# Output pieces split by adding transfers, and narrower first products, in a decoder layer on one core

## The chip, the core and the metric

The kernel runs on one core of one Trainium2 chip. The core has five engines that run side by side and wait for one another by semaphores: TensorE (PE, with its weight loads shown apart as PEld), VectorE (DVE), ScalarE (ACT), GpSimd (POOL) and SyncE (SP, which only issues transfers here). POOL can issue transfers too, among them such as add to what stands in on-chip memory. The metric is the time of one execution on the device in microseconds (us). Before the change the median of three runs is 2339.99 us (2338.28 to 2340.84).

## The reference

One decoder layer on 256 tokens of width 2048, all in float32. What matters here:

```
h = layer_norm(ALPHA * h + 0.5 * swiglu(h, ffn1_w_in, ffn1_w_out), ln1_g, ln1_b)
p = h @ w_in                      # q, k, v, indexer, recurrent branch, gates
merged = g_attn * (dsa_attention(...) @ w_attn_branch) + g_rnn * (rglru_branch(...) @ w_rnn_branch)
h = layer_norm(ALPHA * h + merged @ w_out, ln2_g, ln2_b)
h = layer_norm(ALPHA * h + 0.5 * swiglu(h, ffn2_w_in, ffn2_w_out), ln3_g, ln3_b)

def swiglu(h, w_in, w_out):
    a, b = split(h @ w_in, 2)     # inner width 5632
    return (silu(a) * b) @ w_out
```

Nearly all of the work is products of 256 tokens with weights that are read once. The two FFNs hold most of the weights.

## The kernel before

**Three products for one.** A float32 number is kept as two rounded halves, h (its rounding) and l (the rest). A product of tokens and weights is three products on PE: token h by weight h, token h by weight l, token l by weight h. That is `three` (lines 742 to 745); lines 743, 744 and 745 are therefore the commonest rows of the profile. The tokens are the stationary operand (128 by 128, loaded anew for every product), the weights stream by as 512 or 256 columns.

**Pieces.** All weights form one list of pieces in the order of their use, and `Weights` keeps three places in it: where PE is (`cur`), how far pieces are split into halves (`cur + AHEAD`, 4), and how far they are loaded (8). There are four kinds:

- a plain piece `c` of an FFN's input weights, 1024 columns: twelve products of 512 columns, streamed as two rows of 512;
- a form: a chunk of 2048 columns of the input weights is used in four forms (`p1q3`, `p2`, `q5p7`, `q4p6`), which are sums of its quarters (Strassen's scheme in Winograd's variant). They cost DVE additions (lines 230, 234, 237), and save products. A chunk's forms are 42 products of 256 columns, six (p2) or twelve (the others) a form;
- an output piece `o` of an FFN's output weights, 1024 columns, which fill in between (twelve products of 512 columns);
- pieces of the other stages, of the same shapes.

A piece is split by ACT, which writes h (line 275), and DVE, which subtracts it from the piece and writes l (line 276), into one of five buffers `hl`. A chunk of 2048 columns is loaded into one of three buffers `rf`, other pieces into one of four `raw`.

**Far pieces.** Some output pieces go another way, so that DVE does nothing for them: the far pieces (`far_to`, lines 167 to 187). Their loads are issued when the piece is `EARLY + LOADS` = 16 pieces ahead of PE, their split 12 ahead. ACT writes minus the rounded piece into two tiles `wd` (line 182), POOL issues for each a transfer that reads the piece from memory once more and adds it (line 183), which leaves l; ACT writes h into two further tiles (line 185). In each FFN the output weights are worked off in groups of 4 pieces (k = 0, 2, 4, 6: one segment of the inner width and one quarter of the outputs); far are those with k = 2 and 6 (in the first, shorter segment only k = 2, and for two quarters). That is 34 pieces in each FFN.

**Order.** The order on PE, SP and POOL is that of the program text. On ACT and DVE a scheduler sets it when the kernel is built. An FFN has 22 blocks of 256 inner columns; the last sixteen use four chunks each, with one group of output pieces: three pieces first, then eight forms, the fourth piece, and eight forms. The block's gate (lines 1132 to 1145) is worked off on ACT and DVE while the next block's output pieces run, and its result is turned on PE by four transpositions (line 1151). Other stages mix the same kinds of pieces, with fewer chunks in forms.

`run` (in `blockF`) issues the products of one half form: `three` twice, for two rows of 256 columns. `tokens` calls `three` for the 512-column pieces.

Of the kernel before, what the change touches and what calls it, by code (L numbers as in the profile page):

```python
# [16 lines left out]
S = 256  # L17
# [45 lines left out]
AHEAD = 4  # L63
EARLY = 12
LOADS = 4
FORMS = ("p1q3", "p2", "q5p7", "q4p6")
PIECE = 1024
FAST = (0, 1, 2, 3)
# [69 lines left out]
class Weights:  # L138
# [28 lines left out]
    def far_to(self, i):  # L167


        nc = self.nc  # L170
        while self.far_loaded < len(self.far) and self.far[self.far_loaded] <= i + LOADS:
            k = self.far[self.far_loaded]
            ap = self.pieces[k][0]
            t = self.far_raw[k] = self.pool.tile([P, PIECE], F32, name=f"raw{k}", tag="raw", bufs=RAW_BUFS)
            nc.sync.dma_start(t, ap)
            self.far_loaded += 1
        while self.far_split < len(self.far) and self.far[self.far_split] <= i:
            k = self.far[self.far_split]
            ap, t = self.pieces[k][0], self.far_raw.pop(k)
            h, l = ([self.wide() for _ in range(2)] for _ in range(2))  # L180
            for c in range(2):
                nc.scalar.activation(l[c], t[:, c * 512:(c + 1) * 512], AF.Copy, scale=-1.0)
                nc.gpsimd.dma_start(l[c], ap[:, c * 512:(c + 1) * 512], accum_op=OP.add)
            for c in range(2):
                nc.scalar.activation(h[c], t[:, c * 512:(c + 1) * 512], AF.Copy)
            self.hl[k] = (h, l)
            self.far_split += 1
# [180 lines left out]
def tile_layer(ctx, tc, x_fm, x_tm, pos, f1a, f1o, wA, wki, wB, wG, lru, wab, wrb, wo, f2a, f2o,  # L368
# [46 lines left out]
    def block_pieces(ap, plan, fills=None, fo=None):  # L415
        chunk = {}
        for f, k in plan:
            if f == "c":
                pieces.append((ap[:, k * 512:k * 512 + PIECE], None))
            elif f == "o" and not fo:  # L420
                plain([next(fills)])
            elif f == "o":
                g, nb, k = next(fills)
                if k in (2, 6) and (g or nb >= 2):
                    far.append(len(pieces))
                k += 2 * SEGS[g][0]
                pieces.append((fo[nb][:, k * 512:k * 512 + PIECE], None))
            else:
                if k not in chunk:
                    chunk[k] = ap[:, k * 2048:(k + 1) * 2048]  # L430
                pieces.append((chunk[k], f))
# [30 lines left out]
    for i in range(NR + LAG):  # L462
# [4 lines left out]
        if i >= LAG:  # L467
            g, c = divmod(i - LAG, TPG)
# [273 lines left out]
    def three(ps, xh, xl, w, start, stop):  # L742
        T.matmul(ps, xh, w[0], start=start, stop=False)  # L743
        T.matmul(ps, xh, w[1], start=False, stop=False)  # L744
        T.matmul(ps, xl, w[0], start=False, stop=stop)  # L745

    def tokens(ps, x, t, w, start, stop):
        three(ps, x[:, 0, t * P:(t + 1) * P], x[:, 1, t * P:(t + 1) * P], w, start, stop)

    def eager(hs, ps):  # L750
# [28 lines left out]
    def blockF(x, forms, plan, fill):  # L779
# [14 lines left out]
        for i, (form, k) in enumerate(plan):  # L794
            if i < skip:
                continue
            if form == "o":
                fill()
                continue
            if not c:  # L800
                c = [MM(), MM()]
            start, stop = ([f.get(b) == i for b in range(4)] for f in (first, last))
            if form == "c":
                for j in (k, k + 1):
                    w = W.unit(512)
                    for t in range(2):
                        tokens(c[t], x[j], t, w, start[t] and j == k, stop[t] and j > k)
                continue
            if not e:
                e = [BP(), BP()]  # L810
            c11, c12, c21 = c[0][:, :S], c[0][:, S:], c[1][:, :S]
            p1, p6, p7, q5 = e[0][:, :S], e[0][:, S:], e[1][:, :S], e[1][:, S:]
            fs = [forms[2 * k + r] for r in range(2)]

            def xop(i, t):
                return [tuple(x[4 * k + 2 * r + i][:, a, t * P:(t + 1) * P] for a in range(2)) for r in range(2)]

            def sop(i):
                return [tuple(v[:, i * P:(i + 1) * P] for v in fs[r]) for r in range(2)]

            def run(ps, ops, start, stop):
                for r in range(2):
                    three(ps, *ops[r], W.unit(S), start and r == 0, stop and r == 1)

            if form == "p1q3":
                run(p1, xop(0, 0), start[2], stop[2])
                run(c12, sop(3), start[0], stop[0])
            elif form == "p2":
                run(c11, xop(1, 0), start[0], stop[0])
            elif form == "q5p7":  # L830
                run(q5, sop(0), start[3], False)
                run(p7, sop(2), False, stop[3])
            else:
                run(c21, xop(1, 1), start[1], stop[1])
                run(p6, sop(1), start[2], stop[2])
# [288 lines left out]
    def ffn(x, forms, ln):  # L1124
        def gate(c, e, g, i, lag, plain):
# [20 lines left out]
            for _ in range(lag):  # L1146
                yield
            ps = BP()
            for k in range(2):
                for t in range(2):  # L1150
                    T.transpose(ps[:, k * S + t * P:k * S + (t + 1) * P], z[:, t * 512 + k * P:t * 512 + (k + 1) * P], ident)
# [544 lines left out]
```

## Time and profile before

| | |
|---|---|
| median of the runs | 2339.99 us |
| profiled execution | 2340.27 us, its span 2338.4 us |
| PE busy | 2312.5 us (99%), 15430 products and as many weight loads |
| DVE busy | 2201.5 us (94%) |
| ACT busy | 1560.0 us (67%) |
| POOL busy | 263.4 us (11%) |
| read from memory, written | 507.10 MB, 37.22 MB |
| granted clock of PE | 1.000 |

The first FFN runs to about 705 us, the input projections, attention and the recurrent branch follow, and the second FFN begins at about 1640 us. Rows of the profile name the line, the engine, the operation, what it writes and reads (`out<-in`, numbers of buffers left out) and the size. In rows of groups stand the count, the busy time with the mean of one in ns, and the engine's idle time before them with what ended it. In rows in order of time stand the start, the duration of the row (all of its instructions, where it ends in xN) and, in brackets, idle time before it. A product lasts longer than the step to the next one, since products are pipelined: what a product costs is the step from start to start. Rows of stretches give the busy time of the engines in each, the clock, the share of the DMA engines' time and the rate.

### The profile page before, as it was taken

The page shows a single profiled execution, that of the slowest core. Times are in us where ns is not written, and L with a number is a line of the kernel's source. Part 1 is how long each engine was busy: PE and PEld are TensorE (multiplying, and loading weights), DVE is VectorE, ACT ScalarE, POOL GpSimd, SP SyncE. Part 2 cuts the span into 40 slices and gives each one's busy share as a digit, 9 for nine tenths or more (in the row PEclk, how much of TensorE's full clock was granted, in tenths as well). Part 3 has the DMA queues.
Part 4 walks back from the last instruction along what each step waited for, and adds up shares of the span by engine and source line. Part 5 has one row for each costly group of instructions (what it writes and reads, how often), then busy time and mean ns, then how long its engine had stood idle before and what let it go on. Part 6 is the DMA issues. An engine that isn't in the chain of part 4 may idle for free.

```text
span 2338.4 us, 40427 instructions
## 1 busy us (share of the span) xinstructions
PE 2312.5 (99%) x15430; PEld 2109.4 (90%) x15430; DVE 2201.5 (94%) x3196; ACT 1560.0 (67%) x2273; POOL 263.4 (11%) x368
## 2 busy tenths in 40 slices
PE   9999999999999999999999999999999999999998
PEld 7899999999988999888899998888889999999997
DVE  7999999999999999979887888998999999999997
ACT  7667777777757656556557785555667777777763
POOL 1101111111110000000100001100111111111111
PEclk9999999999999999999999999999999999999999
DMA  9878988888876556554675658655788888888875
GB/s 336 251 238 240 261 250 251 250 256 250 230 244 209 192 187 216 185 189 154 244 239 193 200 182 326 239 198 195 242 275 232 253 255 252 243 252 267 244 221 215
DMA packets 142178, 546.97 MB, mean 234 GB/s; under 512 B 16640, under 2 KB 17280, under 8 KB 117536
## 3 DMA queue, kind: packets, MB, share of 16 engines
q1 hardware_dynamic: 100800, 455.00, 55.1%
q0 software_dynamic: 41040, 89.27, 18.4%
q8 instruction: 120, 1.97, 0.3%
q14 instruction: 74, 0.61, 0.1%
q10 hardware_dynamic: 144, 0.13, 0.0%
HBM read 507.10 MB, written 37.22 MB: 233 GB/s over the span
## 4 chain that ended last, share of the span: by engine, by line
PE 66%; DVE 23%; issue 5%; DMA 3%; ACT 2%; POOL 0%; SPq 0%; ACTq 0%; DVEq 0%; POOLq 0%
PE mm L743 13%; PE mm L745 13%; PE mm L744 13%; DVE hl L276 13%; PE bp L744 5%; PE bp L745 5%; PE bp L743 4%; PE mm L1390 3%; PE mm L1389 3%; PE mm L1391 3%; DVE ws L230 2%; DVE rf L237 2%; DVE rf L234 2%; ACT hl L275 2%; DMA raw<-f1o 1%
## 5 line engine op out<-in xcount | busy, mean ns | idle before, releaser
L275 ACT ACTIVATE hl<-rf 128x1024 fp32r<-128x1024 f32 x573 | 511.3, 912 | 232.9 <-DVE rf L237 119.7
L276 DVE TENSOR_TENSOR hl<-rf,hl 128x1024 fp32r<-128x1024 f32 x573 | 596.9, 1047 | 8.2 <-ACT hl L275 3.8
L276 DVE TENSOR_TENSOR hl<-raw,hl 128x1024 fp32r<-128x1024 f32 (+3 forms) x402 | 474.2, 1196 | 62.2 <-ACT hl L275 61.4
L275 ACT ACTIVATE hl<-raw 128x1024 fp32r<-128x1024 f32 (+3 forms) x402 | 408.4, 1035 | 179.4 <-PE mm L745 82.8
L744 PE MATMUL bp<-hl,sh 128*128 128x256 f32 x1146 | 323.6, 282 | 10.1 <-DVE hl L276 10.1
L743 PE MATMUL bp<-hl,sh 128*128 128x256 f32 x1146 | 320.9, 280 | 0.0
L745 PE MATMUL bp<-hl,sl 128*128 128x256 f32 x1146 | 320.2, 279 | 0.0
L743 PE MATMUL mm<-hl,hs 128*128 128x512 f32 (+1 forms) x800 | 274.5, 343 | 1.6 <-DVE z L1139 0.7
L275 ACT ACTIVATE hl<-ws 128x1024 fp32r<-128x1024 f32 x191 | 202.0, 1058 | 102.7 <-DVE ws L230 71.5
L744 PE MATMUL mm<-hl,hs 128*128 128x512 f32 (+1 forms) x800 | 268.3, 335 | 0.0
L745 PE MATMUL mm<-hl,hs 128*128 128x512 f32 (+1 forms) x800 | 267.9, 335 | 0.1
L230 DVE TENSOR_TENSOR ws<-rf 128x1024 f32<-128x1024 f32 x191 | 233.8, 1224 | 5.4 <-DMA rf<-wrb 1.3
L276 DVE TENSOR_TENSOR hl<-ws,hl 128x1024 fp32r<-128x1024 f32 x191 | 234.2, 1226 | 1.8 <-ACT hl L275 1.7
L744 PEld LDWEIGHTS bp<-hl,sh 128*128 128x128 f32 x1146 | 215.4, 188 | 17.5 <-DVE hl L276 16.3
L745 PEld LDWEIGHTS bp<-hl,sl 128*128 128x128 f32 x1146 | 217.7, 190 | 0.0
L743 PEld LDWEIGHTS bp<-hl,sh 128*128 128x128 f32 x1146 | 215.4, 188 | 1.3
L1389 PE MATMUL mm<-hs,hl 128*128 128x256 f32 x640 | 178.3, 279 | 0.0
L1391 PE MATMUL mm<-hs,hl 128*128 128x256 f32 x640 | 177.8, 278 | 0.0
L1390 PE MATMUL mm<-hs,hl 128*128 128x256 f32 x640 | 177.7, 278 | 0.0
L743 PEld LDWEIGHTS mm<-hl,hs 128*128 128x128 f32 x800 | 150.4, 188 | 19.1 <-issue 2.6
L745 PEld LDWEIGHTS mm<-hl,hs 128*128 128x128 f32 x800 | 151.0, 189 | 16.7 <-DVE hs L937 0.5
L744 PEld LDWEIGHTS mm<-hl,hs 128*128 128x128 f32 x800 | 150.5, 188 | 14.3 <-DVE hl L276 0.2
(360 smaller groups left out, 5897.6 us busy)
## 6 DMA issues: line engine op xcount, KB each, us to landing
rf<-f1a SPq DMA_DIRECT2D x75, 1024.0 KB, 7.7
rf<-f2a SPq DMA_DIRECT2D x75, 1024.0 KB, 7.5
raw<-f1o SPq DMA_DIRECT2D x88, 512.0 KB, 6.6
raw<-f2o SPq DMA_DIRECT2D x88, 512.0 KB, 6.6
raw<-wB SPq DMA_DIRECT2D x80, 512.0 KB, 4.8
raw<-wG SPq DMA_DIRECT2D x54, 512.0 KB, 4.2
ya<-yd POOLq DMA_DIRECT2D x80, 256.0 KB, 7.4
rf<-wA SPq DMA_DIRECT2D x20, 1024.0 KB, 5.5
```

Source lines behind the costliest of these rows:

```text
L230: v.tensor_tensor(t, b[:, 0:4:3], b[:, 1:2].to_broadcast([P, 2, 2, 256]), op=OP.add)
L234: v.tensor_tensor(b[:, 1], t[:, 1], b[:, 0], op=OP.add)
L237: v.tensor_tensor(b[:, 0], b[:, 1], b[:, 2], op=OP.add)
L275: nc.scalar.activation(hp, src, AF.Copy)
L276: self.last = nc.vector.tensor_tensor(lp, src, hp, op=OP.subtract)
L743: T.matmul(ps, xh, w[0], start=start, stop=False)
L744: T.matmul(ps, xh, w[1], start=False, stop=False)
L745: T.matmul(ps, xl, w[0], start=False, stop=stop)
L1389: T.matmul(ps[:, :S], w[0], x[:, 0], start=first, stop=False)
L1390: T.matmul(ps[:, :S], w[0], x[:, 1], start=False, stop=False)
L1391: T.matmul(ps[:, :S], w[1], x[:, 0], start=False, stop=last)
```

## The change

There are two edits. First, output pieces with k = 4 are far pieces too, so that three of four in every group of the longer segments are split by adding transfers, and far pieces are loaded eight pieces ahead of their split instead of four. Second, where a form's products follow products of 512 columns, the first of them is issued as two products of 128 columns, with the same stationary operand. A mark, `after_wide`, is set by `tokens` when it streams 512 columns, and cleared by a form's products and by the transpositions of a gate.

```diff
 LOADS = 4
+FAR_LOADS = 8
@@ far_to
-        while self.far_loaded < len(self.far) and self.far[self.far_loaded] <= i + LOADS:
+        while self.far_loaded < len(self.far) and self.far[self.far_loaded] <= i + FAR_LOADS:
@@ block_pieces
-                if k in (2, 6) and (g or nb >= 2):
+                if k in (2, 4, 6) and (g or nb >= 2):
                     far.append(len(pieces))
@@ beside three
+    after_wide = [False]
+
+    def entry(ps, xh, xl, w, start, stop):
+        n = w[0].shape[1] // 2
+        for c in range(2):
+            T.matmul(ps[:, c * n:(c + 1) * n], xh, w[0][:, c * n:(c + 1) * n], start=start and c == 0, stop=False)
+        T.matmul(ps, xh, w[1], start=False, stop=False)
+        T.matmul(ps, xl, w[0], start=False, stop=stop)
+
     def tokens(ps, x, t, w, start, stop):
+        after_wide[0] = w[0].shape[1] == 512
         three(ps, x[:, 0, t * P:(t + 1) * P], x[:, 1, t * P:(t + 1) * P], w, start, stop)
@@ run, in blockF
-                    three(ps, *ops[r], W.unit(S), start and r == 0, stop and r == 1)
+                    w = W.unit(S)
+                    (entry if after_wide[0] else three)(ps, *ops[r], w, start and r == 0, stop and r == 1)
+                    after_wide[0] = False
@@ gate, before its transpositions
+            after_wide[0] = False
```

The built programs show what this moves. Names below carry the number of the piece, so `hl301` is piece 301; rows of the change have its own line numbers, one to fifteen above the old ones. Piece 298 is the first of a group of output pieces (k = 0), 299 and 300 follow (k = 2 and 4), 301 is the next block's first form, 309 the group's fourth piece.

On PE, at the step from piece 300 to piece 301, before:

```order
L743 MATMUL mm376_5655<-hl300_5601,g303_4349 128x512
L744 MATMUL mm376_5655<-hl300_5601,g303_4349 128x512
L745 MATMUL mm376_5655<-hl300_5601,g303_4349 128x512
L743 MATMUL bp379_5705<-hl301_5628,xs10_132 128x256
L744 MATMUL bp379_5705<-hl301_5628,xs10_132 128x256
```

and now:

```order
L744 MATMUL mm424_5772<-wd413_5589,g335_4433 128x512
L745 MATMUL mm424_5772<-wd415_5591,g335_4433 128x512
L746 MATMUL mm424_5772<-wd413_5589,g335_4433 128x512
L753 MATMUL bp427_5826<-hl301_5745,xs10_132 128x128 x2
L754 MATMUL bp427_5826<-hl301_5745,xs10_132 128x256
```

Piece 300 is read from the tiles `wd` of a far piece, and the first product of piece 301 is two of 128 columns. There are 154 such pairs in the program.

On DVE, at the same place of the list, where a group's output pieces are split, before:

```order
L276 TENSOR_TENSOR hl297_5565<-rf294_5438,hl297_5565 128x1024
L276 TENSOR_TENSOR hl298_5580<-raw298_5514,hl298_5580 128x1024
L276 TENSOR_TENSOR hl300_5601<-raw300_5543,hl300_5601 128x1024
L230 TENSOR_TENSOR ws301_5629<-rf301_5563 128x1024
L1133 TENSOR_TENSOR z374_5645<-z374_5645,bp359_5351 128x256
L276 TENSOR_TENSOR hl301_5628<-rf301_5563,hl301_5628 128x1024
```

and now:

```order
L277 TENSOR_TENSOR hl297_5685<-rf294_5549,hl297_5685 128x1024
L277 TENSOR_TENSOR hl298_5700<-raw298_5637,hl298_5700 128x1024
L231 TENSOR_TENSOR ws301_5746<-rf301_5683 128x1024
L277 TENSOR_TENSOR hl301_5745<-rf301_5683,hl301_5745 128x1024
L235 TENSOR_TENSOR rf301_5683<-ws301_5746,rf301_5683 128x2x256
```

The subtraction for piece 300 is gone; the gate's first addition (z) now stands behind the sums of the form.

On ACT, in the middle of that block, where the far pieces of the next group are split (319, and now 320 as well), before:

```order
L182 ACTIVATE wd386_5807<-raw319_5736 128x512
L182 ACTIVATE wd387_5808<-raw319_5736 128x512
L185 ACTIVATE wd384_5805<-raw319_5736 128x512
L185 ACTIVATE wd385_5806<-raw319_5736 128x512
L275 ACTIVATE hl311_5815<-rf310_5724 128x512
L275 ACTIVATE hl312_5831<-ws310_5795 128x1024
```

and now:

```order
L276 ACTIVATE hl311_5935<-rf310_5846 128x512
L183 ACTIVATE wd434_5927<-raw319_5789 128x512
L183 ACTIVATE wd435_5928<-raw319_5789 128x512
L186 ACTIVATE wd432_5925<-raw319_5789 128x512
L186 ACTIVATE wd433_5926<-raw319_5789 128x512
L183 ACTIVATE wd438_5953<-raw320_5807 128x512
L183 ACTIVATE wd439_5954<-raw320_5807 128x512
L186 ACTIVATE wd436_5951<-raw320_5807 128x512
L186 ACTIVATE wd437_5952<-raw320_5807 128x512
L276 ACTIVATE hl312_5961<-ws310_5915 128x1024
L276 ACTIVATE hl313_5979<-rf310_5846 128x1024
```

Eight conversions of far pieces stand in a row there, ahead of `hl312`, where it had four, ahead of `hl311`. This is so in eight of the 32 blocks; in the others they stand in groups of three to five.

## The prediction

> **What bounds the kernel now.** I read the page first, then the busy time by stretch, the waits of TensorE (PE), and the order of time at a few places.
>
> ```profile
> span 2338.4 us, 40427 instructions
> PE 2312.5 (99%) x15430; PEld 2109.4 (90%) x15430; DVE 2201.5 (94%) x3196; ACT 1560.0 (67%) x2273; POOL 263.4 (11%) x368
> ...
> PE 66%; DVE 23%; issue 5%; DMA 3%; ACT 2%; POOL 0%; SPq 0%; ACTq 0%; DVEq 0%; POOLq 0%
> ```
>
> PE and VectorE (DVE) share the chain that ended last. Which of them binds depends on the stage, so the averages are split by stretch: thirteen equal blocks of the first FFN, fourteen of the second, and the recurrent branch for contrast.
>
> ```profile
> core 0: us, PE busy (x) PEld busy (x) DVE busy (x) ACT busy (x) POOL busy (x), PEclk, DMA share, GB/s
> 249.80:658.80 409.00, 404.57 (x2861) 377.27 (x2861) 407.14 (x494) 292.93 (x409) 69.72 (x82) 1.00 0.85 248
> 1840.90:2280.60 439.70, 435.33 (x3080) 405.88 (x3080) 438.18 (x533) 315.45 (x442) 73.83 (x86) 1.00 0.84 248
> 1100.00:1380.00 280.00, 280.00 (x2225) 267.93 (x2224) 232.58 (x353) 190.73 (x286) 13.94 (x26) 1.00 0.63 212
> ```
>
> In the FFN blocks DVE is busy 407.14 of 409.00 us, while PE is idle for 4.4: DVE sets their period, 409.00/13 = 31.46 us. From 1100 to 1380 PE never rests and DVE has 47 us to spare. So work taken from DVE can pay only in the FFN blocks, and work added to PE costs everywhere unless PE waits.
>
> How much PE waits for DVE stands in the waits, and at one place of each block in the order of time.
>
> ```profile
> PE bp L744 <- DVE hl L276: 10.1, 30, 0.6
> ```
> ```profile
> 375.04 0.28 PE L743 MATMUL bp<-hl,sh 128*128 128x256 f32 x1
> 375.71 0.38 PE L744 MATMUL bp<-hl,sh 128*128 128x256 f32 x1 [0.39 <-DVE hl L276]
> 375.93 0.28 PE L745 MATMUL bp<-hl,sl 128*128 128x256 f32 x1
> ...
> 376.40 0.28 PE L743 MATMUL bp<-hl,sh 128*128 128x256 f32 x1
> ...
> 378.32 0.28 PE L745 MATMUL bp<-hl,sl 128*128 128x256 f32 x1
> 378.44 0.39 PE L743 MATMUL mm<-hl,g 128*128 128x512 f32 x1
> ```
>
> There are thirty waits, one per block, at the last form ahead of the output pieces, 10.1 us of idle time. One costs more than its idle time: the two starts after 375.04 take 0.89 us where two products take 0.23, so 0.66 against 0.39 idle. Taken over the thirty places in the same way, 14.3 us. That is the most that relief of DVE can return here.
>
> **Two pitches of one product.** The seventeen starts from 376.40 to 378.32, behind that wait, are 0.113 us apart. Behind 512 columns the same product goes slower:
>
> ```profile
> 305.02 0.39 PE L745 MATMUL mm<-wd,g 128*128 128x512 f32 x1
> 305.25 0.28 PE L743 MATMUL bp<-hl,xs 128*128 128x256 f32 x1
> 305.36 0.28 PE L744 MATMUL bp<-hl,xs 128*128 128x256 f32 x1
> ...
> 308.66 0.28 PE L745 MATMUL bp<-hl,sl 128*128 128x256 f32 x1
> ```
>
> From 305.25 to 308.66 are 29 steps, 0.1177 us each. The state holds: of 143 stretches of eight and more that begin behind 512 columns, 141 keep the slow pitch to their end (a wait, transpositions, or 512 columns). It is 4.4 ns a product. Transpositions, 128 columns wide, usually end it:
>
> ```profile
> 91.30 0.60 PE L1151 MATMUL bp<-ident,z 128*128 128x128 f32 x4
> 91.65 0.37 PE L743 MATMUL mm<-hl,xs 128*128 128x256 f32 x1
> 91.85 0.28 PE L744 MATMUL mm<-hl,xs 128*128 128x256 f32 x1
> 91.97 0.28 PE L745 MATMUL mm<-hl,xs 128*128 128x256 f32 x1
> ...
> 92.43 0.28 PE L743 MATMUL bp<-hl,sh 128*128 128x256 f32 x1
> ```
>
> **The change, part by part.** *Entries.* 154 products of 256 columns become two of 128 (64 in the 32 four-chunk blocks, two each; 90 elsewhere), each with a weight load of its own, as every product here has (15430 of both on the page). No row shows a rounded product of 128 columns. The nearest are the transpositions above and the plain float32 products of attention:
>
> ```profile
> L1151 PE MATMUL bp<-ident,z 128*128 128x128 f32 x176 | 26.4, 272 | 0.0
> ```
> ```profile
> 1001.05 0.39 PE L1354 MATMUL bp<-hT,hT 128*128 128x128 f32 x2
> 1001.27 0.60 PE L1355 MATMUL bp<-hT,hT 128*128 128x256 f32 x2
> ```
>
> Four transpositions take 0.60 us and one lasts 0.27, so 0.11 a step; two plain products step on in 0.22, again 0.11 each. The upper bound is the slow pitch, 0.118, if each load waits as it does there. Two steps replace one of 0.118: plus 0.100 (from 0.109) to 0.118. I take 0.105, nearer to these rows because of the width: 154 x 0.105 = 16.2 us (15.4 to 18.2), all on PE. The Trainium skill ("TensorE: Matmul & The Clock Gate", section Back-to-back issue gap) gives about 81 ns for a 128-column product in a stream of weight loads and products; by that the pair would add 44 ns, 6.8 us in all, and the sum below would be 2318 us. The trace disagrees for this data: 0.11 us in both rows above.
>
> What the entry may return: from each of the 154 places to the next wait, transposition or 512 columns I count 4,563 products in the trace (the first place at 55.67 us, the last at 2273.04), which at 4.4 ns are 20.0 us. The lower bound is nothing. Behind the transpositions the pitch needs some five products to fall to 0.113 (0.12, 0.12, 0.11 from 91.85), about 2 us over all places: 18. Whether the new pair ends the slow state is the open question. Of 38 waits inside such a stream, a step of chance length, 27 come out at 0.113 (376.40 above) and 11 at 0.118, such as this one:
>
> ```profile
> 407.36 0.39 PE L744 MATMUL bp<-hl,sh 128*128 128x256 f32 x1 [0.52 <-DVE hl L276]
> ...
> 409.71 0.28 PE L745 MATMUL bp<-hl,sl 128*128 128x256 f32 x1
> ```
>
> Transpositions straight behind 512 columns end it in four of seven cases. So I give the pair about six in ten; timing behind 512 columns repeats, so it should be nearly all places or nearly none.
>
> *Three of four pieces.* 32 more pieces (sixteen an FFN, one a block) lose their split on DVE and get four conversions on ScalarE (ACT) and two adding transfers.
>
> ```profile
> L276 DVE TENSOR_TENSOR hl<-raw,hl 128x1024 fp32r<-128x1024 f32 x385 | 464.6, 1223 | 59.1 <-ACT hl L275 58.4
> ...
> 345.46 2.35 DVE L276 TENSOR_TENSOR hl<-raw,hl 128x1024 fp32r<-128x1024 f32 x2
> ...
> 344.19 1.99 ACT L275 ACTIVATE hl<-raw 128x1024 fp32r<-128x1024 f32 x2
> 346.09 1.56 ACT L275 ACTIVATE hl<-rf 128x1024 fp32r<-128x1024 f32 x2
> ...
> 363.30 1.14 ACT L182 ACTIVATE wd<-raw 128x512 fp32r<-128x512 f32 x2
> 364.34 1.14 ACT L185 ACTIVATE wd<-raw 128x512 fp32r<-128x512 f32 x2
> ```
>
> DVE: two subtractions step on in 2.35 - 1.22 = 1.13 us, so a block needs 31.32 - 1.13 = 30.19 us of DVE (407.14/13 = 31.32). PE without its wait needs 31.46 - 0.48 = 30.98, and with two entries 31.19, or 30.9 with the pitch returned. DVE then has 0.7 to 1.0 us to spare in a block, and PE becomes the bound. The wait of 14.3 us goes; I count 80%, 11.4 us, since the relief is small and DVE's gate chain still comes in one burst. ACT: four conversions at 0.52 (364.34 - 363.30 over two) for one of 0.95: plus 1.13 us on 22.5 of 31.46, hidden as a sum. But the order puts eight of them in a row in eight blocks, 4.2 us, ahead of two conversions of a form; elsewhere up to five, 2.6 us.
>
> ```profile
> L182 ACT ACTIVATE wd<-raw 128x512 fp32r<-128x512 f32 x136 | 78.2, 620 | 2.7 <-DMA raw<-f2o 2.1 <-DMA raw<-f1o 0.5
> ...
> L183 POOL DMA_DIRECT2D wd<-f1o x68 | 71.7, 1380 | 335.4 <-ACT wd L182 248.3 <-PE bp L745 65.4 <-DVE g L879 21.7
> ```
> ```profile
> wd<-f1o POOLq DMA_DIRECT2D x68, 256.0 KB, 9.5
> ...
> rf<-f1a SPq DMA_DIRECT2D x75, 1024.0 KB, 7.7
> ```
>
> ACT did wait for these loads, 2.7 us in all; issuing them four pieces earlier (some 5 us) removes that and puts them ahead of chunk loads in SP's queue, whose buffers turn over with DVE and which land in 7.7 us. POOL issues two more transfers a block, 2 x 1.38 us beside 5.3 busy of 31.46: hidden. They land in 9.5 us and are used more than a dozen pieces after their load. The transfers add 0.52 MB to 248 GB/s x 31.46 us = 7.8 MB a block, so the DMA share goes from 0.85 to about 0.91.
>
> Sum against the profiled execution, 2340.27 us (its span of 2338.4 and 1.9 around it; the median of the three runs is 2339.99): + 16.2 - 18 - 11.4 = - 13.2, **2327 us**.
>
> **Rivals.** *The slow pitch stays.* Two loads still bind the two products, and the next 256 columns start as late behind their load as before. For it: eleven of 38 waits, and three of seven transpositions behind 512 columns. Then + 16.2 - 11.4 = + 4.8: **2345 us**, slower than before. It decides once fewer than about 1,000 of the 4,563 products speed up (4.8 us at 4.4 ns).
>
> *DVE keeps waiting, now for ACT.* Behind five or eight conversions in a row DVE's next subtraction starts 2.6 to 4.2 us late, and a block can lose the 0.7 to 1.0 us that was gained. Against it: five buffers of halves let DVE work ahead of PE. Later chunk loads under a fuller DMA would have the same effect. Then only the entries count, + 16.2 - 18 = - 1.8: **2338 us**. With the slow pitch as well, + 16.2: **2356 us**.
>
> *The change does not do what it says.* The mark "behind 512 columns" survives products that are not of that width: ten of the 154 places stand behind transpositions or attention products. That is 1.0 us of cost without a return, inside the rounding of the sum.
>
> *Free entries.* If the second load of the same operand hides, two products of 128 columns cost what one of 256 does at its best, 0.113 by the rows from 376.40, and the 16.2 us fall away: 2311 us. The steps of 0.11 for 128 columns speak against it.
>
> **How the numbers follow.** Forecast 45% (own range 2319 to 2335), slow pitch 25% (2341 to 2350), DVE still waiting with the pitch returned 15%, both failing 10%, free entries 5%. A measurement here tells 0.2%, 4.7 us, from no change. Faster: 45 + 5, less 2 for the forecast's upper edge: 48%. Slower: of the slow pitch 15, both failing 10, and 2 of the third case: 27%. The same: the rest, 25%. The range goes from 2319 to 2349 us; it leaves out both failing, the free entries and the top of the slow pitch.
>
> **What would show it.** After 512 columns: two 128-column rows some 0.11 apart, then 256 columns at 0.113 (right) or 0.118 (the first rival); a first step of 0.06 would be the free entry, one of 0.2 or more, that narrow rounded products are slower than the plain ones at 1001 us, which would end far above the range. In the blocks: no wait for DVE's hl at the last form, and DVE at about 30.2 of 30.9 us. If DVE stays at full share with its waits on ACT grown, the second rival holds. If a DMA stands as releaser of hl or of wd, the transfers are late.

## The result, and the profile after

The changed kernel takes 2371.38 us (median of 4 runs, 2369.78 to 2372.02) where the kernel before takes 2339.14 (4 runs, 2337.77 to 2340.84). The ratio is 1.0135, 95% interval 1.0119 to 1.0152: 32 us slower. The forecast was 2327 us, its range 2319 to 2349.

The page of the changed kernel, and its busy time in the two stretches of FFN blocks shown of before:

```profile
span 2370.1 us, 40871 instructions
...
PE 2323.5 (98%) x15584; PEld 2111.0 (89%) x15584; DVE 2171.8 (92%) x3164; ACT 1595.5 (67%) x2369; POOL 319.0 (13%) x432
...
PE 41%; DVE 16%; ACT 6%; issue 4%; DMA 2%; ACTq 0%; POOL 0%; SPq 0%; DVEq 0%; POOLq 0%
```
```profile
249.80:658.80 409.00, 401.97 (x2860) 372.61 (x2859) 390.47 (x475) 307.82 (x449) 89.48 (x102) 1.00 0.92 264
1840.90:2280.60 439.70, 432.76 (x3079) 401.33 (x3077) 420.27 (x515) 329.92 (x484) 97.72 (x111) 1.00 0.92 265
```

All the work that was to move did move: DVE has 30 us less of it, ACT 36 more, the DMA share is 0.92. But in the first stretch DVE now rests for 18.5 us (1.9 before), and PE for 7.0 (4.4 before). DVE was relieved, and nobody is faster for it. The waits tell who keeps whom. First PE's (engine, line, releaser: us in total, count, longest), then DVE's, then ACT's for the loads of far pieces, all of the changed kernel:

```profile
PE bp L745 <- DVE hl L277: 17.2, 44, 0.9
PE mm L744 <- DVE z L1152: 11.5, 7, 3.2
...
DVE hl L277 <- ACT hl L276: 126.6, 131, 4.3
...
ACT wd L183 <- DMA raw<-f1o: 7.2, 2, 4.9
ACT wd L183 <- DMA raw<-f2o: 7.1, 3, 4.0
```

Before, the DVE row was this:

```profile
DVE hl L276 <- ACT hl L275: 67.0, 88, 2.5
```

PE's waits for DVE's halves grew from 10.1 to 17.2 us, and those for the gate's last addition (`z`) from 0.7 to 11.5. DVE's own waits for ACT nearly doubled, and ACT stands 14.3 us for far pieces that have not landed, where it stood 2.7.

**Where the 32 us lie.** The two traces hold the same products in the same order, a split product being two. So the start of one product can be compared in both. The changed kernel is behind by 0.5 us at 96 us, 8.4 at 192, 14.0 at 704, 18.8 at 1664, 27.0 at 1824, and 31.8 at the end. Three kinds of places lose: the early blocks of each FFN (7.9 and 8.2 us), every fourth of the later blocks (0.9 to 1.4 us each; the others 0.3 or less), and the recurrent branch between the FFNs (4.8 us).

### The profile page after: what moved, and what is told of

Read it like the earlier page. It is cut to its first block, busy times and chain, and to the rows that moved or that the text cites. A ratio compares the mean times of both kernels' runs of the same rounds, so it can differ in the third digit from the quotient of the medians.

```text
span 2370.1 us, 40871 instructions
## 1 busy us (share of the span) xinstructions
PE 2323.5 (98%) x15584; PEld 2111.0 (89%) x15584; DVE 2171.8 (92%) x3164; ACT 1595.5 (67%) x2369; POOL 319.0 (13%) x432
## 4 chain that ended last, share of the span: by engine, by line
PE 41%; DVE 16%; ACT 6%; issue 4%; DMA 2%; ACTq 0%; POOL 0%; SPq 0%; DVEq 0%; POOLq 0%
PE mm L744 9%; PE mm L745 9%; PE mm L746 9%; DVE hl L277 8%; ACT hl L276 2%; PE bp L745 2%; PE bp L746 2%; PE bp L744 2%; DVE ws L231 2%; PE mm L1405 1%; PE mm L1403 1%; PE mm L1404 1%; ACT wd L183 1%; ACT wd L186 1%; DVE rf L238 1%
## 5 line engine op out<-in xcount | busy, mean ns | idle before, releaser
L277 DVE TENSOR_TENSOR hl<-raw,hl 128x1024 fp32r<-128x1024 f32 (+3 forms) x370 | 436.4, 1191 | 67.9 <-ACT hl L276 67.5
L276 ACT ACTIVATE hl<-raw 128x1024 fp32r<-128x1024 f32 (+3 forms) x370 | 377.8, 1034 | 174.6 <-PE mm L746 89.0
L745 PE MATMUL bp<-hl,sh 128*128 128x256 f32 x1113 | 312.0, 280 | 11.9 <-DVE hl L277 11.8
L744 PE MATMUL bp<-hl,sh 128*128 128x256 f32 x1113 | 307.9, 277 | 0.0
L746 PE MATMUL bp<-hl,sl 128*128 128x256 f32 x1113 | 307.7, 276 | 0.0
L745 PEld LDWEIGHTS bp<-hl,sh 128*128 128x128 f32 x1113 | 209.0, 188 | 19.3 <-DVE hl L277 19.0
L744 PEld LDWEIGHTS bp<-hl,sh 128*128 128x128 f32 x1113 | 209.0, 188 | 0.1
L746 PEld LDWEIGHTS bp<-hl,sl 128*128 128x128 f32 x1113 | 209.0, 188 | 0.0
L744 PEld LDWEIGHTS mm<-hl,hs 128*128 128x128 f32 x797 | 150.3, 189 | 24.0 <-issue 6.5
L746 PEld LDWEIGHTS mm<-hl,hs 128*128 128x128 f32 x797 | 150.2, 189 | 17.7 <-DVE hs L892 0.9
L744 PE MATMUL mm<-wd,g 128*128 128x512 f32 (+1 forms) x424 | 164.7, 388 | 0.0
```

The costliest lines, as they stand in the source:

```text
L276: nc.scalar.activation(hp, src, AF.Copy)
L277: self.last = nc.vector.tensor_tensor(lp, src, hp, op=OP.subtract)
```

## The experiments

Every kernel was timed against the kernel before in the same job. All ratios are to that; its median was 2339.1 to 2341.0 us over the jobs, so medians of different jobs are compared to some 2 us at best.

| run | what is in it | median us | ratio, 95% interval |
|---|---|---|---|
| e1 | split first products alone | 2362.6 | 1.0094, 1.0081 to 1.0108 |
| e2 | loads eight ahead alone | 2348.1 | 1.0031, 1.0019 to 1.0042 |
| e3 | third pieces alone | 2339.7 | 0.9996, 0.9987 to 1.0005 |
| e4 | third pieces and loads eight ahead | 2348.5 | 1.0034, 1.0022 to 1.0046 |
| e5 | split products, order of the kernel before | 2344.2 | 1.0011, 1.0003 to 1.0020 |
| e6 | kernel before, order of e1 | 2358.2 | 1.0069, 1.0055 to 1.0082 |
| e7 | split products and third pieces, order of e3 | 2341.4 | 1.0003, 0.9995 to 1.0012 |
| e8 | the whole change, order of e3 | 2345.6 | 1.0019, 1.0010 to 1.0027 |
| e9 | third pieces, far conversions at most two in a row | 2338.0 | 0.9990, 0.9981 to 0.9999 |
| e10 | e9 and the split products | 2341.3 | 1.0001, 0.9992 to 1.0010 |
| e11 | e9 and the split products in the FFNs alone | 2340.1 | 0.9998, 0.9989 to 1.0006 |
| e12 | e9, two far conversions put behind the conversion of a form, 30 places | 2330.9 | 0.9955, 0.9942 to 0.9967 |
| e13 | e12, last additions of the gate first | 2327.3 | 0.9941, 0.9929 to 0.9954 |
| e14 | e13 and the split products in the FFNs alone | 2327.1 | 0.9943, 0.9929 to 0.9956 |
| e15 | the whole change, order of e13 | 2331.1 | 0.9963, 0.9951 to 0.9976 |
| e16 | e15 with loads four ahead | 2330.0 | 0.9960, 0.9947 to 0.9974 |

### The parts one by one

The theory after reading the two traces was that the earlier loads lose some 16 us in the early blocks, that the third pieces lose some 10 to ACT's conversions in a row, and that the split products lose 5 in the branch. Each part was taken alone, by undoing the others:

```diff
 # e1: split first products alone
-FAR_LOADS = 8
+FAR_LOADS = 4
-                if k in (2, 4, 6) and (g or nb >= 2):
+                if k in (2, 6) and (g or nb >= 2):
 # e2: loads alone; e3: third pieces alone (loads 4); e4: both (loads 8)
-                    (entry if after_wide[0] else three)(ps, *ops[r], w, start and r == 0, stop and r == 1)
+                    three(ps, *ops[r], w, start and r == 0, stop and r == 1)
```

> The split first products alone; the output pieces and their loads as before. My theory: the trace of the changed kernel lost 4.8 us from 704 to 1664 us, where no output piece is split by adding transfers and the products cost more than the returned pitch, and in the four-chunk blocks VectorE's 31.3 us of work hides what the pitch returns; so 2340 + 5 = 2345 us (2341 to 2348), with VectorE's waits on ScalarE near those of before (67 us). Rival (the sum over the changed trace, 16.2 paid and 18.4 returned, holds in time as well): 2338 us (2335 to 2340).

> The loads eight pieces ahead alone: pieces 2 and 6 as before, no split products. My theory: the loss before 192 us and from 1696 to 1824 us (8.4 + 8.0 us), where no third piece exists yet, comes from the earlier loads: ScalarE gets the conversions of a piece ahead of others and stands for a load that has not landed (4.85 us at 95.7 us in the changed trace); so 2340 + 16 = 2356 us (2350 to 2359), lost in these two stretches. Rival (the loss there is due to the new order of VectorE's and ScalarE's work that the split products bring): 2338 to 2342 us.

> Three of four pieces alone, loads four pieces ahead as before, no split products. My theory: ScalarE's conversions in a row hold VectorE 1 to 2.3 us per block, which returns what the missing subtraction freed (1.13 us), and more in the eight blocks with eight in a row (1.1 to 1.3 us each, 10 us in all): 2350 us (2345 to 2354), VectorE's waits on ScalarE about 110 us. Rival (late loads or a fuller DMA made the loss, and four pieces ahead leave them later still): 2360 us and more, with a DMA as releaser of wd. A second rival (the conversions cost nothing and VectorE's relief pays): 2330 us.

> The change without its split products: three of four pieces, loads eight ahead. My theory adds the parts: 2340 + 16 + 10 = 2366 us (2360 to 2370). Rival (the split products and the order they bring are the main loss): 2340 to 2350 us.

The theory fell in its main number. The split products alone cost 22.4 us, not 5, the loads 8.0, not 16, and the third pieces nothing, where 10 were counted. e4, the last two together, takes what e2 takes, in the range that its rival gave (the order that the split products bring is the main loss). In e1 the slow pitch is gone as in the changed kernel: summed over all steps of 2 to 9 ns above 113.35 ns between two products of 256 columns it was 24.6 us before and is 6.6. PE pays 16.2 us and gets 18.1 back, and still the kernel is 22 us slower. Most of it comes in equal parts, 0.36 us in each later block, and some 3.5 us at the end of each FFN, so something other than PE's own work costs there.

What e1 changes beside PE is not in its text. The order on ACT and DVE is set by a scheduler when the kernel is built, and it comes out otherwise when PE has 154 products more. By the two recorded orders (of e5 and e6 below), at least 283 of 2,223 instructions of ACT and 438 of 3,180 of DVE stand elsewhere in e1 than in the kernel before, although neither engine has one instruction more or less.

### The order held fast

So the order was made a thing of its own. The instructions of ACT and DVE are emitted in the same sequence in both kernels. The order that the scheduler made of one was recorded as a list of places, and laid on the other by dependencies that fix the order of issue on one engine and wait for nothing else (shortened):

```python
    for e, text in ORDERS.items():
        run = [mine[k + int(d)] for k, d in enumerate(moved)]   # the recorded order
        for (m, a), (n, b) in zip(run, run[1:]):
            tc.add_manual_dep(b, a.name, issue_order_only, reason="order")
```

The lines of these kernels stand lower by the lines added; `L774` in e6 and `L775` in the others are `L743` of the kernel before. In the traces, ACT and DVE have the rows of e1 in e6, those of the kernel before in e5, and those of e3 in e8, each in the same sequence.

> The split first products on TensorE, with ScalarE's and VectorE's instructions held in the order that they have in the kernel before (by dependencies that cost no wait). Theory now: the split products alone cost 22.4 us because they shift the scheduler's order of VectorE and ScalarE, and TensorE itself pays 16.2 us and gets 18.4 back; then 2340 us (2336 to 2344). Rival (the price is on TensorE: two weight loads more at each place make it late everywhere, whatever the order): 2356 to 2363 us.

> The kernel before, nothing split and nothing added, with ScalarE's and VectorE's instructions in the order that the scheduler gives them beside the split products. Theory (the order alone costs): 2355 to 2365 us. Rival (the order is harmless, the split products cost): 2337 to 2343 us.

> Split products and three of four pieces, loads four ahead, ScalarE and VectorE in the order of the third pieces alone (2339.7 us). Theory (with the order held, TensorE's pitch is a gain where VectorE no longer sets the period): 2330 to 2338 us. Rival (VectorE, which waits for ScalarE's conversions in a row, still sets the period): 2338 to 2342 us. If the price is on TensorE: 2355 us and more.

> The whole changed kernel, loads eight ahead included, with ScalarE and VectorE in the order of the third pieces alone with loads four ahead. Theory (the loads' 8 us, too, come from the order, which sets the conversions of a piece ahead of others before the piece has landed): within 2 us of the run without the earlier loads. Rival (the earlier loads themselves delay chunk loads in SP's queue): 6 to 10 us above that run.

This settles the main cause. e6 has the instructions of the kernel before and not one more, and takes 2358.2 us: the order alone costs 17 us. e5 has the split products in the old order and costs 3.2. The whole change in the order of the third pieces (e8) costs 4.7 us, in the order that its own text gives it 32. So about 27 of the 32 us are the order of ACT's and DVE's work. The dependencies themselves cost nothing that these runs tell: the price of the order of e1 is 17.3 us where that order is laid on (e6 against the kernel before), and 18.4 where the old one is laid on (e1 against e5). e7 shows that the third pieces and the split products together gain nothing in this order either: the rival was right, DVE, with its waits for ACT, still sets the period there. e8 lies 4.2 us above e7, between the two expectations, and their intervals touch; the loads' own price is taken up again at the end.

What the order does can be seen in a later block. ACT and DVE in order of time, first before:

```profile
363.04 0.36 ACT L878 ACTIVATE g<-bp 128x256 fp32r<-128x256 f32 x1
```
```profile
360.94 1.23 DVE L276 TENSOR_TENSOR hl<-ws,hl 128x1024 fp32r<-128x1024 f32 x1
362.07 0.42 DVE L879 TENSOR_TENSOR g<-bp,g 128x256 fp32r<-128x256 f32 x1
```

and in e6:

```profile
365.84 0.39 ACT L909 ACTIVATE g<-bp 128x256 fp32r<-128x256 f32 x1 [0.99 <-DVE g L910]
366.12 1.14 ACT L182 ACTIVATE wd<-raw 128x512 fp32r<-128x512 f32 x2
367.16 1.14 ACT L185 ACTIVATE wd<-raw 128x512 fp32r<-128x512 f32 x2
368.20 1.05 ACT L275 ACTIVATE hl<-ws 128x1024 fp32r<-128x1024 f32 x1
```
```profile
361.86 1.22 DVE L276 TENSOR_TENSOR hl<-ws,hl 128x1024 fp32r<-128x1024 f32 x1
363.11 1.23 DVE L230 TENSOR_TENSOR ws<-rf 128x1024 f32<-128x1024 f32 x1
364.25 1.22 DVE L276 TENSOR_TENSOR hl<-rf,hl 128x1024 fp32r<-128x1024 f32 x1
365.39 0.42 DVE L910 TENSOR_TENSOR g<-bp,g 128x256 fp32r<-128x256 f32 x1
...
369.28 1.23 DVE L276 TENSOR_TENSOR hl<-ws,hl 128x1024 fp32r<-128x1024 f32 x1 [0.21 <-ACT hl L275]
```

DVE makes the gate's product (`g`) two operations later than before. ACT, whose queue is in order, waits 0.99 us for it, and behind that wait stand four conversions of a far piece and then the conversion of a form, for which DVE in turn waits. DVE sets the period here, so each of its gaps is a loss: from 256 to 640 us, twelve blocks, e6 falls back by 4.3 us, 0.35 a block. Over the thirteen blocks of the first stretch, the same products in both, it takes 4.5 us more: DVE's late starts behind a conversion of ACT sum to 5.0 us, where they were 2.0, and 1.5 us are lost because a sum of DVE now stands directly behind the one whose result it reads (1.26 us from start to start at 357.65, where 1.14 is usual, as from 363.11 to 364.25). At the end of the second FFN the gate's last addition stands late in DVE's order, PE stops for 2.3 us, and some 3.5 are lost there.

The same shows in the early blocks, in e2 (and in the changed kernel, where it is longer). The order puts the conversions of a far piece ahead of two conversions of forms, as if its load had landed. In e2 it was issued right behind a chunk's load; its issue was done at 89.93 us, and it landed 9.0 us later. ACT in e2:

```profile
98.96 0.63 ACT L183 ACTIVATE wd<-raw 128x512 fp32r<-128x512 f32 x1 [3.35 <-DMA raw<-f1o]
99.50 1.56 ACT L276 ACTIVATE hl<-rf 128x1024 fp32r<-128x1024 f32 x2
```

In the changed kernel, ACT and DVE at the same place:

```profile
100.59 0.63 ACT L183 ACTIVATE wd<-raw 128x512 fp32r<-128x512 f32 x1 [4.85 <-DMA raw<-f1o]
101.12 1.56 ACT L276 ACTIVATE hl<-rf 128x1024 fp32r<-128x1024 f32 x2
```
```profile
102.20 1.23 DVE L277 TENSOR_TENSOR hl<-rf,hl 128x1024 fp32r<-128x1024 f32 x1 [4.28 <-ACT hl L276]
```

DVE loses 4.28 us to a transfer that neither it nor PE needs yet. With the order held, ACT's waits for these loads are gone: of the 14.3 us 0.8 are left in e8 and none in e15.

### Why relief of DVE paid nothing, and then did

With the order held, one thing was still open: in e3 and e7 each of 32 blocks has 1.13 us less on DVE, and the time does not move. In an ordinary later block of e3, ACT and then DVE:

```profile
301.06 1.14 ACT L183 ACTIVATE wd<-raw 128x512 fp32r<-128x512 f32 x2
302.10 1.14 ACT L186 ACTIVATE wd<-raw 128x512 fp32r<-128x512 f32 x2
303.14 0.62 ACT L276 ACTIVATE hl<-rf 128x512 fp32r<-128x512 f32 x1
303.67 1.14 ACT L183 ACTIVATE wd<-raw 128x512 fp32r<-128x512 f32 x2
304.71 1.14 ACT L186 ACTIVATE wd<-raw 128x512 fp32r<-128x512 f32 x2
305.75 1.05 ACT L276 ACTIVATE hl<-ws 128x1024 fp32r<-128x1024 f32 x1
```
```profile
305.12 0.68 DVE L238 TENSOR_TENSOR rf<-rf 128x512 f32<-128x512 f32 x1
306.83 1.23 DVE L277 TENSOR_TENSOR hl<-ws,hl 128x1024 fp32r<-128x1024 f32 x1 [1.03 <-ACT hl L276]
```

DVE is done at 305.8 and waits 1.03 us for a conversion that stands behind eight of far pieces, with one short one among them. Most of what was freed, 1.13 us, is given back at one place. In every fourth block of the changed kernel the eight stand without a break (the last two are shown), and the wait is 2.29 us:

```profile
281.25 1.14 ACT L186 ACTIVATE wd<-raw 128x512 fp32r<-128x512 f32 x2
282.30 1.05 ACT L276 ACTIVATE hl<-ws 128x1024 fp32r<-128x1024 f32 x1
```
```profile
283.37 1.23 DVE L277 TENSOR_TENSOR hl<-ws,hl 128x1024 fp32r<-128x1024 f32 x1 [2.29 <-ACT hl L276]
```

Over the thirteen blocks of the first stretch, product by product the same ones, 13 x 1.13 = 14.7 us were freed. DVE's late starts behind ACT's conversions there grew from 2.0 us to 13.9 in e3 and 19.1 in the changed kernel. The little that e3 gains in these blocks, 2.2 us, its early blocks lose again (2.4 us from 96 to 192 us).

The recorded order of e3 was therefore changed by a rule: behind two far conversions the next conversion of a form goes first (shortened).

```python
        if far(x): waiting.append(x)
        else:
            out.append(x)
            if form(x): row = 0
        while waiting and row < 2:
            out.append(waiting.pop(0)); row += 1
```

> Three of four pieces, loads four ahead, nothing split (2339.7 us), with ScalarE's order changed: after two conversions of far pieces the next conversion of a form goes first, where four to eight stood in a row. Theory (VectorE, relieved of 1.13 us a block, loses 1.0 to 1.7 us a block to ScalarE's conversions in a row, 98 us of waits in all; once these go, TensorE's waits for VectorE's halves go too, 5.6 us idle, some 8 us in time): 2331 to 2336 us, VectorE's waits on ScalarE under 60 us. Rival (the wait only moves to the next conversion, or the far pieces come late): 2338 us or more.

> The same with the split first products. Theory (once VectorE does not set the period, the pitch that they return shows in the FFN's blocks, some 3 us, and the branch still pays about 2 to 3): 2330 to 2336 us, within 2 us of the run without them. Rival (VectorE still sets the period): 2 to 4 us above that run.

> The same with the split first products in the two FFNs alone (86 of the 154 places; the branch between has 18 to 31 products behind a place, 24 pay for one). Theory: 1 to 3 us below the run with all of them, 2328 to 2334 us. Rival (places do not matter beside the waits): the same as that run.

e9 came out at the rival's edge, 2338.0 us: 1.7 us below e3, which the two intervals do not tell from nothing. DVE's waits for ACT fell only from 98.2 to 93.8 us, where the theory had under 60. e10 is 3.3 us above it, as the rival had it, and e11 lies between the two, not told apart from either. The wait had moved, as the rival said, to one place in the block. In e9 two far conversions and two copies of a finished output piece (`yd`) stand ahead of a form:

```profile
305.27 1.14 ACT L186 ACTIVATE wd<-raw 128x512 fp32r<-128x512 f32 x2
306.31 1.07 ACT L1219 ACTIVATE yd<-mm 128x512 f32<-128x512 f32 x2
307.27 1.58 ACT L276 ACTIVATE hl<-rf 128x1024 fp32r<-128x1024 f32 x2
```
```profile
308.36 1.23 DVE L277 TENSOR_TENSOR hl<-rf,hl 128x1024 fp32r<-128x1024 f32 x1 [0.59 <-ACT hl L276]
```

e12 moves the two far conversions behind that form, at 30 places. e13 also puts the gate's last additions, at the end of each FFN, ahead of the subtraction of a piece that arrives late (2 places). e14 adds the split products in the FFNs.

> Three of four pieces, loads four ahead, at most two far conversions in a row (2338.0 us), and where two of them stood ahead of the two copies of a finished output piece and the conversion of a form behind those, they now stand behind that conversion (30 places). Theory (one wait of 0.6 us of VectorE for ScalarE is left in a block, just there, ahead of the chain that ends at the last form; without it TensorE's wait there shrinks by as much as TensorE leaves room, 0.2 to 0.3 us a block): 2331 to 2336 us. Rival (VectorE's chain through the block is full, or the wait moves on): 2337 to 2340 us.

> The same, and at the end of each FFN the gate's last additions go ahead of the subtraction of a piece that arrives late (2 places; the kernels with three pieces stand 1.2 to 2.7 us there). Theory: 2 to 4 us below the run without that. Rival (the late piece holds TensorE as well): within 1 us of it.

> The same with the split first products in the two FFNs. Theory (VectorE is no longer late, so the pitch shows): 2 to 4 us below the run without them, 2326 to 2333 us. Rival (VectorE or the buffers still set the period): the same or 1 to 2 us above.

e12 takes 2330.9 us, 7 below e9, as the theory said. PE's waits at the last form, 10.1 us before, were still 4.8 in e9 and are gone in e12 but for one:

```profile
PE bp L776 <- DVE hl L277: 4.8, 17, 0.6
```
```profile
PE bp L776 <- DVE hl L277: 0.6, 1, 0.6
```

e13 takes 2327.3, another 3.6 below. The intervals of the two overlap; PE's waits for the gate's last addition fall from 4.8 to 1.8 us. In e13's first stretch of blocks PE does not rest at all:

```profile
249.80:658.80 409.00, 409.00 (x2905) 383.71 (x2904) 400.82 (x490) 310.18 (x451) 91.44 (x107) 1.00 0.93 269
```

From 256 to 640 us, 12.2 blocks, e13 gains 6.3 us on the kernel before, 0.52 a block: the period is 30.94 us and PE sets it. DVE is busy 400.82/409 of that, 30.3 us. Its late starts behind ACT are not gone, 9.3 us in the thirteen blocks, but they no longer reach PE.

e14 shows nothing beside e13 (2327.1 against 2327.3), as the rival said, and here the theory missed. The pitch is there: the sum of slow steps falls by 17.2 us, from 27.8 to 10.6. The 86 pairs cost 9 to 10 us of it. Most of the rest is small steps of PE that are 9 to 150 ns too long (3.1 us more, the pairs' own left out) and stops of over 150 ns (2.7 us more). Six of these stops, 1.3 us, lie in the first FFN's thirteen blocks, each at a product that waits for DVE's half; e13 has none there. So DVE, 98% busy, is the likely source, but no run separates that.

At last the whole change was given the order of e13, and the same with loads four ahead:

> The whole changed kernel (all 154 split products, three of four pieces, loads eight ahead), with ScalarE and VectorE in the hand-set order of the fastest run (2327.3 us without split products and earlier loads). Theory (the order is what made the change slow; entries cost 2 to 3 us in the branch, the earlier loads 4 us): 2332 to 2336 us. Rival (the earlier loads do not matter once the order is held): 2328 to 2331 us. If something beside the order made the change slow: 2345 us and more.

> The same with loads four ahead as before: all 154 split products and three of four pieces in the hand-set order. Theory (the branch's 68 places cost 1 to 3 us above the run with the split products in the FFNs alone, 2327.1 us): 2328 to 2330 us; its distance to the run with loads eight ahead is the loads' own price, 3 to 5 us. Rival: no distance.

The change as it was written, to the last instruction, takes 2331.1 us in that order, 0.4% faster than the kernel before; in the scheduler's order it takes 2371.4. The loads' own price, e15 against e16, is 1.1 us, which the intervals do not tell from nothing, and the rival is right there. In e3's order it was 4.2 (e8 against e7). If either holds for e2 too, 4 to 7 of its 8.0 us are the order that the loads brought. All 154 split products cost 2.7 us by the medians (e16 against e13, two jobs, whose intervals overlap), 4.1 by the traces. The fastest kernel is e13 or e14, 13 us below the one before; that needs the third pieces and the order, and neither the split products nor the earlier loads.

## Why the prediction was wrong, point by point

**What bounds the kernel: right.** DVE sets the period of the FFN blocks, and PE would take over at 30.9 to 31.0 us if DVE were relieved. e13 shows that period, 30.94, with DVE at 30.3 where 30.19 was worked out.

**Entries, 16.2 us: right in the sum, not in the steps.** Behind 512 columns the changed kernel steps like this:

```profile
281.74 0.39 PE L746 MATMUL mm<-wd,g 128*128 128x512 f32 x1
281.97 0.33 PE L753 MATMUL bp<-hl,xs 128*128 128x128 f32 x2
282.03 0.27 PE L753 MATMUL bp<-hl,xs 128*128 128x128 f32 x1
282.14 0.33 PE L754 MATMUL bp<-hl,xs 128*128 128x256 f32 x1
282.31 0.28 PE L755 MATMUL bp<-hl,xs 128*128 128x256 f32 x1
282.43 0.28 PE L744 MATMUL bp<-hl,xs 128*128 128x256 f32 x1
...
284.01 0.28 PE L746 MATMUL mm<-hl,xs 128*128 128x256 f32 x1
```

The row at 282.03 is the second product of the pair by itself. From the pair's first start (281.97) to the third product (282.31) it is 0.34 us, where one product of 256 columns took two steps of 0.118 to get there. That is plus 0.105 for a pair, the value taken. But the steps are not the two of 0.11 that it was worked out from. The first is 0.06 (so in 143 of the 154 pairs), which the prediction had named as the sign of a free entry; the second is 0.11, and the product behind the pair takes 0.17 instead of 0.118. Half of the price is paid one product later, and that the sum agrees is luck.

**Pitch returned, 18 us: right in size, wrong in worth.** From 282.43 to 284.01 are 14 steps of 0.113 us. Of 140 stretches that begin behind a pair, 134 run at the fast pitch; before, 141 of 143 ran at the slow one. The sum of slow steps fell by 18.4 us. But with the order held, the split products cost 3.2 us (e5) instead of returning 1.8. What failed here is the sum over all places. In e5's two stretches of FFN blocks the pairs cost 6.2 us over the fast pitch and the slow steps fall by 7.9, but DVE sets the period and the time moves by 0.5 us at most. From 704 to 1664 us, where the branch lies, 68 pairs cost 9.0 us and the slow steps fall only from 10.0 to 5.4, and e5's trace falls 3.7 us behind. The first part of the prediction had said that work added to PE costs there; the sum did not apply it.

**The wait for DVE, minus 11.4 us: right for the work, wrong for this order.** With ACT in a suitable order, partly set by hand, the third pieces brought 13.0 us (e13), 3.6 of them with the two places at the FFNs' ends. In the scheduler's order they brought nothing (e3). "ACT hidden as a sum" was true and beside the point; the eight conversions in a row, 4.2 us, stood in the text, and the second rival named just what happened: DVE's next subtraction starts late. The rival was given 15% and, as its worst, the loss of the 0.7 to 1.0 us that had been won. The change lost more, because each gap of DVE counts in full where DVE sets the period, and because the order made gaps in blocks that have no third piece.

**Loads four pieces earlier: wrong in sign.** They were to remove 2.7 us of ACT's waits, and ACT's waits for these loads became 14.3. An earlier issue in SP's queue did not make them land in time for the place that the scheduler then gave the conversions. With the place held, ACT hardly waits for them, and the earlier loads bring nothing: they cost 4.2 us in one order and 1.1 in the other, and the intervals of each two runs overlap.

**The missing term: the step that failed.** The order of ACT and DVE was shown in the part on the change, with the gate's additions behind other work and the conversions in a row, and then used as if it moved only the rows shown. No term and no rival priced the new order of the two engines as a whole, though the split products, which have nothing on either engine, moved hundreds of instructions there. The order was put at nothing, without a reason. It is the largest term: 17 us by e6 alone, 27 of the 32 by e8, and 40 between the changed kernel and e15. That is why the worst rival, 2356, was passed by 15 us. In the hand-set order the sum stands 4 us off (e15, 2331.1, against 2327), most of which is the split products' net price; in e3's order 19 us off (e8, 2345.6). So the sum held only for an order that the scheduler does not make.

## What to carry to other kernels

Where a scheduler sets the order of an engine, an edit on another engine is also an edit there; price it by itself, by laying the old order on the new kernel and the new order on the old one. An in-order engine that feeds the bound is never "hidden as a sum": look for what stands directly ahead of the one instruction that the bound waits for, and put work with slack (far conversions, copies) behind it. Work taken from the bounding engine shows in the time only when the wait that reaches the next engine is gone: here the first half of the reordering brought nothing that the intervals tell, and one more place in the block 7 us.

## What the runs showed of the hardware that was not expected

A stop of PE costs more than itself. In the changed kernel PE waits 3.20 us for the gate's addition before 1728.07, and the products behind it are 0.43 us apart instead of 0.23:

```profile
1728.07 0.77 PE L744 MATMUL mm<-hl,hs 128*128 128x512 f32 x1 [3.20 <-DVE z L1152]
1728.63 0.63 PE L745 MATMUL mm<-hl,hs 128*128 128x512 f32 x1
```

By stretches (length, busy time of PE, its weight loads, DVE, ACT and POOL, then the granted clock):

```profile
1718.00:1724.50 6.50, 6.50 (x36) 5.57 (x35) 4.10 (x5) 4.17 (x8) 0.00 (x0) 1.00 1.04 344
...
1728.00:1733.50 5.50, 5.43 (x14) 4.35 (x14) 5.22 (x6) 2.17 (x3) 2.66 (x3) 0.50 0.98 274
```

The granted clock was 0.50 for 5.5 us, which is 12 steps of 512 columns at 0.2 us more, 2.4 us on top of the stop. In e1 a stop of 2.09 us before 1718.92 was followed by eight such steps (granted clock 0.54 from 1718.8 to 1722), and one of 2.10 us in the changed kernel before 683.69 by none (1.00 from 683.6 to 690). The Trainium skill ("TensorE: Matmul & The Clock Gate", section "Part 1: The HAM clock gate (the "warmup" mystery)") says that the clock is halved after an idle window of about 3.4 us which runs freely. The half clock agrees with the rows, the length does not: stops as short as 2.09 us were enough here.

The other is the weight of order by itself: e15 and the changed kernel have the same instructions on every engine, and one takes 40 us, 1.7%, less.
